# An encoder layer in float32 on one core: another weight split, other queues and another order in its seven-product stages

## Chip, cores and metric

The kernel runs on 1 core of one Trainium2 chip. The metric is the device time of one execution in microseconds; smaller is better. The engines are named as in the profile: PE (TensorE), DVE (VectorE), ACT (ScalarE), POOL (GpSimd) and SP (SyncE, which here only issues DMAs).

## What is computed

One layer of an encoder trunk over 1024 tokens of width 2048: RMSNorm, one input projection, grouped-query attention (8 query heads, 2 key heads) beside a bidirectional state-space part, then three products that this change is about, an output norm and a per-layer gate.

```python
y_ssm = jax.nn.gelu(y_ssm).astype(x.dtype)
glu = y_ssm @ w_glu[i] + b_glu[i]                       # (1024,1024) @ (1024,2048)
y_ssm = glu[..., :D_SSM] * jax.nn.sigmoid(glu[..., D_SSM:])
y_ssm = y_ssm * jax.nn.silu(gate_s)
h = h + jnp.concatenate([y_attn, y_ssm], axis=-1) @ w_out[i]   # (1024,2048) @ (2048,2048)
gate = jax.nn.sigmoid(rms_norm(h, norm_ple[i]) @ w_ple_gate[i])
h = h + gate * (p[i] @ w_ple_proj[i])
```

## The kernel before, in words

Data lie transposed: features on partitions, tokens along the free axis, in halves of 512. A float32 product is made of three matmuls on parts rounded to a shorter type: each operand is split into a high part H and a low part L = x - H, and HH + HL + LH is summed in PSUM. `split` (line 306) does it: ACT copies x to H with rounding (line 310; with a scale, line 313), DVE subtracts (line 311; line 314). `split_pool` (line 316) does both on POOL.

The program is written out in one order by hand, and each engine runs its instructions in that order. Helpers that run in pieces (generators) are put in a list with `bg`; `tick` (line 270) runs each of them one piece further, and takes one entry from the queue of fills `fq` if it is due. In the stages below the queue is `paced`: only three ticks of five take one (line 277). `put` (line 1090) issues the DMA of a moving tile `st` and appends its fill (its split) to be due `wait` ticks later.

After attention, `back` (line 1426) runs three stages of eight units: the gated product with w_glu (units 0 to 7), then w_out over the attention half (units 8 to 15), then over the other half (units 16 to 23). A unit multiplies a 2 x 2 block of weights, two tiles of 128 output features, with seven products instead of eight (Strassen's scheme in Winograd's form). The moving sides of the seven products are halves of the source or sums of them that `t_make` (line 1118) makes on POOL beforehand; `put_product` (line 1152) puts the four tiles of one. The weight sides are four blocks A11 to A22 and four sums of them: `sw_prep` (line 438) splits the next weights, three products ahead of use (`sw_next`, line 468), and `sw_sum` (line 432) makes the sums on POOL. `unit` (line 1165) runs 7 x 4 x 3 = 84 matmuls (lines 1176 to 1178) with a tick after each four-fold step's three matmuls, so four ticks per product and 28 per unit. After each product its PSUM tile (`pr`, four buffers) goes to `u_glu` (line 1191) or `u_out` (line 1238), which add it up: DVE adds at lines 1209 to 1226 and 1256 to 1281, POOL adds of SBUF tiles at lines 1210, 1221 and 1248. In the third stage `close` also squares each result (ACT, line 1264) and sums the squares (POOL, line 1265).

A `hook` after each product loads ahead: after product 6 of a stage's seventh unit and products 0 to 5 of its eighth, the next stage's products are put one by one. In the last unit it is the 14 first tiles of the gate stage (`put_h`), and the first three gate weights (`w_dma`, line 384; split by `w_split`, line 390).

The gate stage (`gate`, line 1392) multiplies two token halves with 16 blocks each: 48 matmuls `pg` (lines 1302 to 1304) and 6 matmuls `pp` per block. Before the second half its 16 tiles are put: nine in blocks 12 to 14, seven after the matmuls of block 15.

The stages begin while attention ends: `run` puts product 0 of the first stage six blocks before attention's last one, products 1, 2 and 3 later, products 4 to 6 after attention. Its loads share SP's queue with the store of the last attention output (line 1083).

Of the kernel before, what the change touches and what calls it, by code (L numbers as in the profile page):

```python
# [9 lines left out]
F32 = mybir.dt.float32  # L10
# [228 lines left out]
class Kernel:  # L239
# [30 lines left out]
    def tick(self):  # L270
        self.nt += 1
        for g in list(self.bgs):
            try:
                next(g)
            except StopIteration:
                self.bgs.remove(g)
        if self.fq and self.fq[0][0] <= self.nt and (not self.paced or self.nt % 5 in (0, 2, 4)):
            self.fill(*self.fq.pop(0)[1:])
# [153 lines left out]
    def sw_sum(self, u, o, a, b, op):  # L432

        if o not in self.sr and isinstance(o[1], str):
            self.sr[o] = self.wp.tile([128, 512], F32, name="wraw", tag="wraw", bufs=3)
        self.nc.gpsimd.tensor_tensor(self.sr[o], self.sr[a], self.sr[b], op)

    def sw_prep(self, g):
# [6 lines left out]
        L = self.wp.tile([128, 4, 128], F32R, name="wL", tag="wL", bufs=4)  # L445
        self.split(H, L, self.sr[src].rearrange("p (k m) -> p k m", m=128))
        self.shl[g] = (H, L)
# [703 lines left out]

    def put_product(self, X, i, s, src, **kw):
        for k in range(4):
            a = {
                0: src[k][:, 0:512],
                1: src[k + 4][:, 0:512],
                2: self.d_t[s][k][1][:, 512:1024],
                3: self.d_t[s][k][0][:, 512:1024],
                4: self.d_t[s][k][0][:, 0:512],
                5: src[k + 4][:, 512:1024],  # L1160
                6: self.d_t[s][k][1][:, 0:512],
            }[i]
            self.put(X, (i, k), a, **kw)

# [26 lines left out]
    def u_glu(self, n):  # L1191
# [27 lines left out]
        nc.vector.scalar_tensor_tensor(u1, ps, bv, u1, ALU.add, ALU.add)  # L1219
        nc.scalar.activation(g1, g1, AF.Sigmoid, bias=bg)  # L1220
        nc.gpsimd.tensor_tensor(v(g1), v(g1), rev(gs[:, h1]), ALU.mult)
        ps = yield
        nc.vector.tensor_tensor(u1, ps, u1, ALU.add)
        nc.vector.tensor_tensor(v(gs[:, h1]), rev(u1), rev(g1), ALU.mult)
        ps = yield
        nc.vector.tensor_tensor(u2, ps, u2, ALU.add)
        nc.scalar.activation(u2, u2, AF.Sigmoid, bias=bg)
        self.bg(self.u_glu_end(n, gs, v(gs[:, h0]), rev(v0), rev(u2)))
        yield

    def u_glu_end(self, n, gs, o, a, b):
        yield
        self.nc.vector.tensor_tensor(o, a, b, ALU.mult)
        for _ in range(5):
            yield
        self.nc.sync.dma_start(self.d_ms[n], gs)

    def u_out(self, m, src, dst, sq):
# [14 lines left out]
        def close(x, h, ps):  # L1253
# [3 lines left out]
            if not sq:  # L1257
                return
            acc = self.xsq[:, h]
            if m == 0 and x is r[0 if h is h0 else 1]:  # L1260
                nc.scalar.activation(acc, x[:, h], AF.Square)
            else:
                s2 = self.t2k("tq")
                nc.scalar.activation(s2, x[:, h], AF.Square)
                nc.gpsimd.tensor_tensor(acc, acc, s2, ALU.add)

# [24 lines left out]

    def mm_half(self, ps, nk, xs):

        nc = self.nc
        for k in range(nk):
# [9 lines left out]
            if k % 2:  # L1305
                self.tick()

    def h_rstd(self):
# [88 lines left out]
    def gate(self, hf, hg, nhg):  # L1397
# [5 lines left out]
        for n in range(16):  # L1403
# [7 lines left out]
            if hf == 0 and 12 <= n < 15:  # L1411
                self.put_h(nhg, 1, range(3 * n - 36, 3 * n - 33))
            self.mm_half(pg, 16, hg)
            if hf == 0 and n == 15:
                self.put_h(nhg, 1, range(9, 16))
            pp = self.psC("pp")
# [7 lines left out]
    def back(self, X):  # L1424
# [6 lines left out]
        hg = {}  # L1431
# [4 lines left out]
        for n, (s, u, thread) in enumerate(units):  # L1436

            def hook(i):
                if u < 7:
                    if u == 6 and i == 6:  # L1440
                        if s < 2:
                            self.put_product(nX, 0, s + 1, stages[s + 1][0])
                        else:
                            self.put_h(hg, 0, range(5))
                elif s < 2:
                    if i < 6:
                        self.put_product(nX, i + 1, s + 1, stages[s + 1][0], wait=8)
                else:
                    if i < 2:
                        self.put_h(hg, 0, range(5 + 4 * i, 9 + 4 * i), wait=8)  # L1450
                    elif i == 2:
                        self.put_h(hg, 0, [13], wait=8)
                    elif i == 3:
                        self.w_end = len(self.wq)
                        for _ in range(2):
                            self.w_dma()
                    elif i == 5:
                        self.w_dma()
                        for _ in range(2):
# [25 lines left out]
    def run(self):  # L1485
# [68 lines left out]
        for b in self.attention():  # L1554
# [9 lines left out]
            elif b == NB - 4 or b == NB - 2:  # L1564
                self.put_product(X, (b - NB + 6) // 2, 0, self.d_y2, pool=True, wait=2)
            elif b == NB + 1:
                self.put_product(X, 3, 0, self.d_y2, wait=2)
            elif b == NB + 2:
                self.sw_prep(0)
            elif b == NB + 3:  # L1570
                self.sw_prep(1)
        for i in range(4, 7):
            self.put_product(X, i, 0, self.d_y2, wait=3)
        self.back(X)
# [97 lines left out]
```

## Time and profile before

| | us |
|---|---|
| three timed runs | 2172.76, 2176.38, 2178.88 (median 2176.38) |
| the profiled execution's own time | 2172.48 |
| its span, first to last instruction | 2170.6 |
| mean granted TensorE clock in it | 0.986 |

Times in the profile count from the span's start. Attention ends and unit 0 begins at 1226.8, the second stage at 1389.5, the third at 1553.2; the last unit's matmuls end at about 1729.5, and the gate stage follows to the end. A granted clock of 1.00 is 2.4 GHz, 0.5 is 1.2 GHz. A matmul's modelled length overlaps the next one, so a busy PE is not a PE at its peak.

### The profile page before, as it was taken

To read this page: it belongs to the slowest core of one execution; us is meant where nothing else is said; L and a number is where in the kernel's file an instruction comes from. 1 tells how busy PE (TensorE), PEld (TensorE's weight loads), DVE (VectorE), ACT (ScalarE), POOL (GpSimd) and SP (SyncE) were. 2 spreads that over 40 slices of the span, in tenths; PEclk is the share of its full clock that TensorE was granted. 3 is DMA by queue.
4 is the path that set the end of the run, shared out by engine and by line. 5 is a ranking of instruction groups with operands and counts; after the bars stand their busy time and mean duration, and the time that the engine had idled before them with its cause. 6 is when DMAs were issued, how large, how long until landed. Compare 5 with 4: busy or idle time off the path is not lost. (4 is left out here: it accounts for less than half of the span.)

```text
span 2170.6 us, 29380 instructions
## 1 busy us (share of the span) xinstructions
PE 2076.4 (96%) x10140; PEld 1717.4 (79%) x10140; DVE 1496.1 (69%) x2394; ACT 798.7 (37%) x1454; POOL 965.1 (44%) x837
## 2 busy tenths in 40 slices
PE   8999999999999999999999899999989799999996
PEld 6888878888878888778888778778767678877885
DVE  7654787778878787749999867866766643455434
ACT  7111322222322222447777632522433343344332
POOL 0143456555556565504312467498478711221222
PEclk9999999999999999999999999999999999999998
DMA  5323223233232232554312545757835444455433
GB/s 214 92 99 101 80 83 105 82 99 87 88 101 80 82 109 72 173 190 153 126 40 79 187 173 174 271 201 257 293 121 170 155 136 127 128 185 165 142 114 126
DMA packets 183123, 296.47 MB, mean 137 GB/s; under 512 B 28352, under 2 KB 78656, under 8 KB 182720
## 3 DMA queue, kind: packets, MB, share of 16 engines
q1 hardware_dynamic: 181824, 292.51, 41.5%
q8 instruction: 80, 1.31, 0.3%
q10 hardware_dynamic: 1152, 2.10, 0.3%
q14 instruction: 67, 0.55, 0.1%
HBM read 211.37 MB, written 77.92 MB: 133 GB/s over the span
## 5 line engine op out<-in xcount | busy, mean ns | idle before, releaser
L311 DVE TENSOR_TENSOR wL<-wraw,wH 128x512 fp32r<-128x512 f32 (+1 forms) x352 | 305.3, 884 | 360.5 <-ACT wH L310 355.2
L310 ACT CAST wH<-wraw 128x512 fp32r<-128x512 f32 (+1 forms) x352 | 205.3, 598 | 344.1 <-DMA wraw<-in_w_gate_dram 98.1
L1177 PE MATMUL pr<-st,wH 128*128 128x512 f32 x672 | 267.3, 398 | 15.6 <-DVE st L311 15.6
L1176 PE MATMUL pr<-st,wH 128*128 128x512 f32 x672 | 266.0, 396 | 12.0 <-DVE cx L1256 7.9
L1178 PE MATMUL pr<-st,wL 128*128 128x512 f32 x672 | 265.3, 395 | 0.2
L1302 PE MATMUL pg<-st,wH 128*128 128x512 f32 x512 | 202.0, 394 | 9.2 <-ACT wH L310 7.9
L1303 PE MATMUL pg<-st,wH 128*128 128x512 f32 x512 | 201.4, 393 | 2.7 <-DVE st L314 2.6
L1304 PE MATMUL pg<-st,wL 128*128 128x512 f32 x512 | 200.8, 392 | 0.3 <-DVE wL L311 0.2
L1330 POOL TENSOR_TENSOR h<-cx,tz 128x512 f32<-128x512 f32 x31 | 40.4, 1303 | 297.5 <-DVE tz L1328 297.5
L1177 PEld LDWEIGHTS pr<-st,wH 128*128 128x128 f32 x672 | 127.8, 190 | 49.0 <-DVE st L311 23.2
L1176 PEld LDWEIGHTS pr<-st,wH 128*128 128x128 f32 x672 | 127.9, 190 | 44.6 <-issue 8.7
L1178 PEld LDWEIGHTS pr<-st,wL 128*128 128x128 f32 x672 | 128.2, 191 | 28.0 <-DVE wL L311 1.9
L311 DVE TENSOR_TENSOR wL<-sraw,wH 128x512 fp32r<-128x512 f32 x120 | 120.2, 1002 | 41.2 <-ACT wH L310 41.1
L892 ACT COPY ks<-kp 16x224 f32<-16x224 f32 x32 | 10.7, 335 | 335.3 <-DVE ks L891 208.7
L1248 POOL TENSOR_TENSOR cx<-cx,tz 128x512 f32<-128x512 f32 x64 | 102.1, 1606 | 64.5 <-DVE tz L1277 54.6
L1302 PEld LDWEIGHTS pg<-st,wH 128*128 128x128 f32 x512 | 96.8, 189 | 32.2 <-ACT wH L310 8.7
L1303 PEld LDWEIGHTS pg<-st,wH 128*128 128x128 f32 x512 | 96.9, 189 | 25.2 <-DVE st L314 5.0
L1304 PEld LDWEIGHTS pg<-st,wL 128*128 128x128 f32 x512 | 96.7, 189 | 21.8 <-DVE wL L311 1.8
L765 POOL TENSOR_TENSOR tab<-pa 128x512 f32<-128x512 f32 x32 | 41.4, 1292 | 159.5 <-DVE r L900 159.5
L310 ACT CAST wH<-sraw 128x512 fp32r<-128x512 f32 x120 | 73.0, 616 | 94.2 <-PE pr L1177 59.7
L574 PE MATMUL zga<-hH,wH 128*128 128x512 f32 x256 | 104.4, 408 | 0.0
L574 PE MATMUL zgs<-hH,wH 128*128 128x512 f32 x256 | 102.7, 401 | 0.6 <-ACT wH L310 0.6
(370 smaller groups left out, 5406.4 us busy)
## 6 DMA issues: line engine op xcount, KB each, us to landing
wraw<-in_w_in_dram SPq DMA_DIRECT2D x144, 256.0 KB
wraw<-in_w_gate_dram SPq DMA_DIRECT2D x128, 256.0 KB
sraw<-in_w_out_dram SPq DMA_DIRECT2D x64, 256.0 KB
st<-d_t SPq DMA_DIRECT2D x48, 256.0 KB
sraw<-in_w_glu_dram SPq DMA_DIRECT2D x32, 256.0 KB
cx<-in_xT_dram SPq DMA_DIRECT2D x16, 512.0 KB
d_p<-cx SPq DMA_DIRECT2D x16, 512.0 KB
cx<-d_p SPq DMA_DIRECT2D x16, 512.0 KB
```

The costliest lines, as they stand in the source:

```text
L310: nc.scalar.copy(H, src)
L311: nc.vector.tensor_tensor(L, src, H.bitcast(F32), ALU.subtract)
L574: nc.tensor.matmul(ps[h], H[:, kk, :], rH[:, s], start=(k == 0), stop=False)
L765: gp.tensor_tensor(out, x[:, :, None, :].to_broadcast(sh), pw[:, :, :, None].to_broadcast(sh), ALU.mult)
L1176: nc.tensor.matmul(ps, H[:, k], x[0], start=(k == 0), stop=False)
L1177: nc.tensor.matmul(ps, H[:, k], x[1], start=False, stop=False)
L1178: nc.tensor.matmul(ps, L[:, k], x[0], start=False, stop=(k == 3))
L1248: nc.gpsimd.tensor_tensor(x[:, h], x[:, h], u, ALU.add)
L1302: nc.tensor.matmul(ps, H[:, k % 4], x[0], start=(k == 0), stop=False)
L1303: nc.tensor.matmul(ps, H[:, k % 4], x[1], start=False, stop=False)
L1304: nc.tensor.matmul(ps, L[:, k % 4], x[0], start=False, stop=(k == nk - 1))
L1330: eng.tensor_tensor(hp, ho, t, ALU.add)
```

## The change

`sw_prep` copies H of each weight once more, on ACT into a PSUM tile `hp` (in the two buffers that attention's scores used), and DVE subtracts that copy instead of H. `sw_sum` runs on DVE for the weights of units 18 to 22. Fills are taken at four ticks of five, and in the second and third stage's puts four of the 28 tiles are split on POOL. In `u_glu` sigmoid and what follows it become pieces of their own, a tick or more apart; in `close` the square comes two ticks after the addition and its sum a tick later. At the start, products 3 and 4 are put during attention's last blocks, product 5 after it and product 6 after unit 0's first product. At the end the three gate weights are loaded from unit 22's last product on, and the seven last tiles of the second half are put within block 15.

```diff
-        if self.fq and self.fq[0][0] <= self.nt and (not self.paced or self.nt % 5 in (0, 2, 4)):
+        if self.fq and self.fq[0][0] <= self.nt and (not self.paced or self.nt % 5 != 4):
...
-        self.nc.gpsimd.tensor_tensor(self.sr[o], self.sr[a], self.sr[b], op)
+        eng = self.nc.vector if 18 <= u < 23 else self.nc.gpsimd
+        eng.tensor_tensor(self.sr[o], self.sr[a], self.sr[b], op)
...
-        self.split(H, L, self.sr[src].rearrange("p (k m) -> p k m", m=128))
+        raw = self.sr[src].rearrange("p (k m) -> p k m", m=128)
+        hp = self.ps.tile([128, 4, 128], F32, name="hp", tag="A", bufs=2)
+        self.nc.scalar.copy(H, raw)
+        self.nc.scalar.copy(hp, H.bitcast(F32))
+        self.nc.vector.tensor_tensor(L, raw, hp, ALU.subtract)
...
-    def put_product(self, X, i, s, src, **kw):
+    def put_product(self, X, i, s, src, share=False, **kw):
...
+            if share:
+                kw["pool"] = (4 * i + k) % 7 == 6
...
         nc.vector.scalar_tensor_tensor(u1, ps, bv, u1, ALU.add, ALU.add)
-        nc.scalar.activation(g1, g1, AF.Sigmoid, bias=bg)
-        nc.gpsimd.tensor_tensor(v(g1), v(g1), rev(gs[:, h1]), ALU.mult)
+        def half_1():
+            yield
+            nc.scalar.activation(g1, g1, AF.Sigmoid, bias=bg)
+            yield
+            nc.gpsimd.tensor_tensor(v(g1), v(g1), rev(gs[:, h1]), ALU.mult)
+            for _ in range(5):
+                yield
+            nc.vector.tensor_tensor(v(gs[:, h1]), rev(u1), rev(g1), ALU.mult)
+        def half_0():
+            yield
+            nc.scalar.activation(u2, u2, AF.Sigmoid, bias=bg)
+            yield
+            yield
+            nc.vector.tensor_tensor(v(gs[:, h0]), rev(v0), rev(u2), ALU.mult)
+            for _ in range(5):
+                yield
+            nc.sync.dma_start(self.d_ms[n], gs)
+        self.bg(half_1())
...
             nc.vector.tensor_tensor(x[:, h], ps, x[:, h], ALU.add)
             if not sq:
                 return
+            yield
+            yield
...
                 nc.scalar.activation(s2, x[:, h], AF.Square)
+                yield
                 nc.gpsimd.tensor_tensor(acc, acc, s2, ALU.add)
...
-            self.mm_half(pg, 16, hg)
             if hf == 0 and n == 15:
-                self.put_h(nhg, 1, range(9, 16))
+                self.mm_half(pg, 16, hg, lambda k: k < 15 and self.put_h(nhg, 1, [9 + k // 2], wait=3))
...
+                if n == 0 and i == 0:
+                    self.put_product(X, 6, 0, self.d_y2)
...
+                            self.w_end = len(self.wq)
+                            self.w_dma()
                             self.put_h(hg, 0, range(5))
...
-                        self.put_product(nX, i + 1, s + 1, stages[s + 1][0], wait=8)
+                        self.put_product(nX, i + 1, s + 1, stages[s + 1][0], wait=8, share=True)
...
+                        if i == 1:
+                            self.w_dma()
+                            self.w_dma()
...
-                    elif i == 3:
-                        self.w_end = len(self.wq)
-                        for _ in range(2):
-                            self.w_dma()
                     elif i == 5:
-                        self.w_dma()
...
+            elif b == NB:
+                self.put_product(X, 3, 0, self.d_y2, wait=2)
             elif b == NB + 1:
-                self.put_product(X, 3, 0, self.d_y2, wait=2)
+                self.put_product(X, 4, 0, self.d_y2, wait=2)
...
-        for i in range(4, 7):
-            self.put_product(X, i, 0, self.d_y2, wait=3)
+        self.put_product(X, 5, 0, self.d_y2, wait=6)
```

## Rows read from the trace of the kernel before

**Rows 1.** Page, part 1: busy time of each engine over the whole span.
```profile
PE 2076.4 (96%) x10140; PEld 1717.4 (79%) x10140; DVE 1496.1 (69%) x2394; ACT 798.7 (37%) x1454; POOL 965.1 (44%) x837
```

**Rows 2.** Windows: stretch, length; PE, PEld, DVE, ACT, POOL busy (instructions); clock; DMA.
```profile
1226.80:1275.30 48.50, 42.06 (x171) 32.81 (x170) 35.20 (x46) 19.09 (x33) 23.43 (x17) 0.93 0.58 207
...
1275.30:1389.50 114.20, 114.20 (x505) 94.64 (x504) 86.76 (x105) 41.32 (x73) 72.30 (x48) 1.00 0.62 210
...
1389.50:1438.90 49.40, 42.91 (x169) 31.82 (x168) 38.73 (x50) 17.97 (x33) 28.81 (x19) 0.97 0.60 207
...
1553.20:1607.10 53.90, 44.32 (x170) 33.42 (x169) 39.40 (x47) 22.16 (x40) 32.09 (x22) 0.91 0.52 181
...
1645.20:1729.50 84.30, 78.97 (x337) 61.97 (x335) 53.01 (x61) 32.61 (x57) 66.85 (x47) 1.00 0.52 172
...
1729.50:1759.40 29.90, 20.55 (x75) 13.94 (x74) 18.46 (x35) 11.06 (x19) 8.93 (x6) 0.83 0.36 119
...
1931.70:1944.00 12.30, 12.30 (x55) 10.14 (x54) 4.34 (x7) 3.95 (x7) 2.58 (x2) 1.00 0.45 128
...
1944.00:1962.30 18.30, 14.81 (x64) 10.68 (x62) 13.07 (x28) 11.53 (x19) 2.59 (x2) 1.00 0.57 204
```

**Rows 3.** Waits of PE, whole kernel: total us, times, longest.
```profile
PE pr L1177 <- DVE st L311: 15.6, 16, 2.4
...
PE pr L1176 <- DVE cx L1256: 7.9, 7, 3.1
...
PE pg L1302 <- ACT wH L310: 7.9, 2, 6.9
```

**Rows 4.** Lines 311 and 1256, units 0 to 23: ns shortest/median/longest.
```profile
L311 DVE TENSOR_TENSOR wL<-sraw,wH x119: 673/992/1814, 1228.0 to 1725.0; 128x512 fp32r<-128x512 f32 x119
...
L1256 DVE TENSOR_TENSOR cx<-pr,cx x64: 673/678/693, 1406.4 to 1740.3; 128x512 f32<-128x512 f32 x64
```

**Rows 5.** The window around unit 8, and DVE's timeline in it.
```profile
1375.10:1418.20 43.10, 36.61 (x149) 26.86 (x148) 41.06 (x55) 22.33 (x42) 19.80 (x11) 1.00 0.77 269
...
1388.42 5.19 DVE L311 TENSOR_TENSOR st<-st 128x512 fp32r<-128x512 f32 x3
...
1398.71 0.69 DVE L311 TENSOR_TENSOR wL<-sraw,wH 128x512 fp32r<-128x512 f32 x1 [1.30 <-ACT wH L310]
...
1402.83 1.88 DVE L311 TENSOR_TENSOR st<-st 128x512 fp32r<-128x512 f32 x3
```

**Rows 6.** ACT copies, SBUF to SBUF and PSUM to SBUF, as rows 4.
```profile
L310 ACT CAST wH<-sraw x118: 601/621/626, 1227.5 to 1724.4; 128x512 fp32r<-128x512 f32 x118
...
L1206 ACT COPY tz<-pr x8: 576/578/587, 1234.0 to 1373.8; 128x512 f32<-128x512 f32 x8
```

**Rows 7.** POOL: split, sum of weights (as rows 4); window of unit 22.
```profile
L318 POOL CAST st<-st x12: 609/618/811, 1181.6 to 1219.2; 128x512 fp32r<-128x512 f32 x12
...
L319 POOL TENSOR_TENSOR st<-st x12: 1262/1287/1300, 1182.3 to 1219.9; 128x512 fp32r<-128x512 f32 x12
...
L436 POOL TENSOR_TENSOR sraw<-sraw x24: 1275/1728/1758, 1225.9 to 1710.5; 128x512 f32<-128x512 f32 x24
...
1684.90:1705.70 20.80, 19.86 (x86) 15.58 (x86) 12.13 (x15) 6.72 (x12) 17.96 (x13) 1.00 0.51 166
```

**Rows 8.** SP's timeline at unit 0: start, length of issue, what.
```profile
1229.02 0.32 SPq L1083 DMA_DIRECT2D d_o<-ga  x1
...
1238.35 2.30 SPq L429 DMA_DIRECT2D sraw<-in_w_glu_dram  x4
```

**Rows 9.** Timelines of ACT and of SP where the gate stage begins.
```profile
1735.36 0.63 ACT L1264 ACTIVATE tq<-cx 128x512 f32<-128x512 f32 x1 [6.06 <-DVE cx L1256]
...
1750.36 0.62 ACT L310 CAST wH<-wraw 128x512 fp32r<-128x512 f32 x1 [8.11 <-DMA wraw<-in_w_gate_dram]
...
1740.45 0.92 SPq L1189 DMA_DIRECT2D d_h<-cx  x2
...
1745.36 0.39 SPq L387 DMA_DIRECT2D wraw<-in_w_gate_dram  x1
```

More of the change, by code (lines that the diff above doesn't have):

```diff
@@ L1219, in u_glu @@
         nc.vector.scalar_tensor_tensor(u1, ps, bv, u1, ALU.add, ALU.add)
-        nc.scalar.activation(g1, g1, AF.Sigmoid, bias=bg)
-        nc.gpsimd.tensor_tensor(v(g1), v(g1), rev(gs[:, h1]), ALU.mult)
+        def half_1():
[16 more added lines that the diff above has]
+        self.bg(half_1())
         ps = yield
         nc.vector.tensor_tensor(u1, ps, u1, ALU.add)
-        nc.vector.tensor_tensor(v(gs[:, h1]), rev(u1), rev(g1), ALU.mult)
         ps = yield
         nc.vector.tensor_tensor(u2, ps, u2, ALU.add)
-        nc.scalar.activation(u2, u2, AF.Sigmoid, bias=bg)
-        self.bg(self.u_glu_end(n, gs, v(gs[:, h0]), rev(v0), rev(u2)))
+        self.bg(half_0())
         yield
[L1231 to L1236, printed above, removed]
     def u_out(self, m, src, dst, sq):
@@ L1290, in u_out, with mm_half @@
         yield
-    def mm_half(self, ps, nk, xs):
+    def mm_half(self, ps, nk, xs, each=None):
         nc = self.nc
@@ L1306, in mm_half @@
                 self.tick()
+                if each:
+                    each(k)
     def h_rstd(self):
@@ L1412, in gate @@
                 self.put_h(nhg, 1, range(3 * n - 36, 3 * n - 33))
-            self.mm_half(pg, 16, hg)
             if hf == 0 and n == 15:
-                self.put_h(nhg, 1, range(9, 16))
+                self.mm_half(pg, 16, hg, lambda k: k < 15 and self.put_h(nhg, 1, [9 + k // 2], wait=3))
+            else:
+                self.mm_half(pg, 16, hg)
             pp = self.psC("pp")
```

## Prediction, made blind

> **What bounds the kernel now.** I read the page first. TensorE is busy for 96% of the span [rows 1], so time can only come from the places where it isn't fed or runs at a lower clock. I looked for those next, in the windows by unit [rows 2]. A unit is 84 matmuls; the reader is to see that six units in a row take 114.2 us, 19.03 each, at a granted clock of 1.00, and that the other windows exceed that: units 0 and 1 by 48.5 - 38.1 = 10.4 us, units 8 and 9 by 11.3, units 16 and 17 by 15.8, units 20 to 23 by 84.3 - 76.1 = 8.2. The first two blocks of the gate stage's halves are long as well: 29.9 against 12.3 us for a plain block (part of it the 20 matmuls that only this block has), and 18.3 against 12.3. So at most about 45.7 + 14 + 5 = 65 us is to be had, 3% of the kernel. Part of it is clock: 1 - granted clock is 0.07, 0.03, 0.09 and 0.17 of the first three pairs and the gate window, or 3.4 + 1.5 + 4.9 + 5.1 = 15 us that TensorE ran at 1.2 GHz, each time after waits.
>
> Third, TensorE's waits say for whom [rows 3]: VectorE's splits of the moving operand (st), VectorE's additions that empty PSUM (cx), and at the gate ScalarE's wH. So VectorE's queue is late just where a stage begins. Why shows the view of its durations [rows 4]: the same 128x512 subtraction takes 0.68 us at best and up to 1.8 when both inputs lie in SBUF, and never over 0.69 when one lies in PSUM. In the stretch around unit 8 [rows 5] VectorE is busy 41.06 of 43.10 us with 55 instructions; undisturbed ones follow each other every 0.60 us (three in 1.88), so 33 us of it is work and 8 us is waiting inside instructions (three st splits in 5.19).
>
> **The change, part by part.** *Subtraction from PSUM.* Each of the 168 weight splits gets a ScalarE copy of H to PSUM. No row shows a SBUF to PSUM copy; its neighbours are SBUF to SBUF at 0.62 us and PSUM to SBUF at 0.58 [rows 6]. I take 0.6 and bound it by 0.5 and 1.2 (twice a neighbour): 7 per unit are 4 us (3.5 to 8.4) of ScalarE, which is busy 41.3 of 114.2 us in six units, 6.9 per unit. It stays idle half of the time, so in plain units the copy costs nothing. VectorE's part falls from about 1.0 us (median 0.99) to 0.68: 7 x 0.3 = 2 us less per unit. The chain to the weights grows by one copy and one hand-over, under 1.5 us, while a split is made three products ahead, 3 x 19.03/7 = 8.2 us.
>
> The port itself: VectorE instructions with two SBUF inputs lengthen to what GpSimd's instruction beside them takes [rows 4, 7], those with one do not. The Trainium skill, in "SBUF — State Buffer", section "Who interferes with whom", says that such an instruction and a GpSimd one that reads SBUF exclude each other for the whole instruction. The trace agrees for VectorE (1.81 us at most, against 1.76 for a GpSimd sum [rows 7]). By that rule it also speaks against two other parts, the fills shared to GpSimd and the sums given to VectorE, since each keeps two SBUF inputs; if each of the eight GpSimd instructions of the shared fills blocked in full (1.29 us instead of the 8/11 = 0.73 us found below), the transitions would lose about 4 us more apiece.
>
> *Fills at four ticks of five instead of three, 4 of 28 on GpSimd, sigmoid issued apart.* At a stage's end 28 fills are put for the next stage. A tick is a quarter product, 0.68 us. Counted from unit 7's first tick, the first fill is due at tick 6; at 0.6 per tick the last is issued at tick 52, at 0.8 at tick 41, and TensorE wants it at tick 55, 33 us after tick 6. Before, 55 instructions stood ahead of it: 33 us of work plus 8 inside waits plus 2 of gaps make 43, 10 late, and 11.3 was lost. After, 24 fills, 9 weight splits and 11 others are 44 x 0.60 = 26.4 us; waits inside I take as 9 (15 GpSimd instructions instead of 11, but 26 of 44 exposed instead of 42 of 55), gaps 1.5: 37, some 4 late. The other limit is the emptying of PSUM: an addition issued at tick 40 frees the bank that TensorE wants at tick 48, 5.4 us later, and VectorE is then 9 to 11 us behind: 4 to 6 late. I take 5.5 left at unit 8 and 7 at unit 16: gains 6 and 9. Bounds: nothing left (11 and 16), or no gain, if the waits inside grow as far as the work shrinks. The four GpSimd fills are 4 x (0.62 + 1.29) = 7.6 us [rows 7] beside its own work; they have 14 ticks or more of room. The sigmoid a tick later only reorders ScalarE's queue: nothing by itself.
>
> *Start of unit 0.* SyncE's queue stands at the last attention store until 1229.02, and the first weights of unit 1 go out only at 1238.35, behind products 4 to 6, twelve loads, and a gate tile: 0.7 us each [rows 8]. After, product 3's loads are issued one block and product 4's two steps earlier, ahead of that store; product 5's four remain behind it, and product 6's four pass behind the first weights. So four loads and one gate tile stand ahead of those weights, eight loads fewer, 5 us sooner. Products 3 and 4 are now split among the last attention blocks, where ScalarE waits for TensorE anyway; what they delay if not is the last transposes, by 0.6 us each at most for 5 fills. I take 8 of the 10.4 (5 to 10).
>
> *Sums on VectorE and squares later, third stage.* GpSimd is busy 17.96 of 20.8 us in unit 22 [rows 7], above 19.03 with any wait, and VectorE's additions wait for it, TensorE for them (7.9 us, [rows 3]). Taking four sums of 1.3 to 1.8 us [rows 7] away leaves 12. VectorE, at 12.1 us there, gets 4 x 0.7 to 1.8 and loses 2: 13 to 17, still under 19. Behind a sum that waits for its load stand the additions that empty PSUM; the loads go out more than two products ahead. Squares two ticks later no longer hold ScalarE's wH. Gain 6.5 of 8.2 (0 to 8).
>
> *Gate.* ScalarE's first gate wH stands behind a square that waited 6.06 us for VectorE's addition, and SyncE sends the fourth weight tile at 1745.36, behind stores that wait for the last additions until 1740.45 [rows 9]. After, the square comes behind the wH, the 14 fills are issued some 10 ticks sooner, and three weight loads go out a unit earlier (one ahead of five st loads, two ahead of four: 0.4 us of issue each, in a queue that afterwards stands until 1740.45 anyway). What is late next is that fourth tile: store, two reloads and its landing remain one chain, 1740.45 to 1750.36 at its split, some 10 us behind the last addition, against 12 x 3 x 0.227 = 8.2 us of matmuls that can run before it. Gain 6.5 (3 to 12).
>
> *Second half.* Seven loads and fills spread over block 15 instead of after it. The block that wants them takes 18.3 instead of 12.3 us, with nine matmuls more [rows 2], so some 4 to 5 us of it are waits; I take 3.5 (0 to 5).
>
> **The sum.** 8 + 6 + 9 + 6.5 + 6.5 + 3.5 = 39.5 us. The profiled execution took 2172.5 us (span 2170.6), 3.9 below the median 2176.4; taken from the median: 2137.
>
> **Rivals.** (1) *VectorE stays the bound at the transitions*, since fills on GpSimd and fills on VectorE block each other: 15 us of gain fall away, at worst some of unit 0's: 2152 to 2165. For it: 8 us inside waits today; against it: fewer exposed instructions and earlier issue. (2) *Slower: ScalarE loses its lead.* The PSUM copies have two buffers, freed by VectorE's subtraction two splits earlier, so ScalarE can't run further ahead of VectorE. If each of the 28 fills then pays a ScalarE to VectorE hand-over like the 1.30 us gap of [rows 5], about 1 us, that is 28 us per transition and 12 at unit 0: 68 against 39.5 gained, 2205. It decides once VectorE is over two products, 5.4 us, late throughout; against it, two splits ahead still means some six fills in hand. (3) *No change*: the subtraction stays long although H is in PSUM, and the lateness moves elsewhere; 64 of 64 additions with a PSUM input under 0.70 us speak against it: 2170 to 2180.
>
> **How the numbers follow.** The forecast, each term within its bounds, 2119 to 2150: 0.70. Rival 1: 0.19. Rival 3: 0.06. Rival 2: 0.05. The range is 2118 to 2161: below lies only the case that nearly all 65 us go, above rivals 2 and 3 and the rest of 1. About 0.3%, 6.5 us, can be told from no change in this kernel: faster 0.89, same 0.06, slower 0.05.
>
> **What would show it.** Right: weight subtractions at 0.68 us with no tail; units 0, 8 and 16 at 20 to 25 us instead of 28 to 34; units 20 to 23 at 19; the gate's first block near 23; no half clock at unit 0 and shorter ones elsewhere; VectorE still without pause around units 7 to 9. Wrong: subtractions still up to 1.8 us; ScalarE idle before its PSUM copies for VectorE; a plain unit, such as 3 or 12, above 19.1; or long waits for VectorE's sums in units 18 to 22.

## The result, and the profile after

The changed kernel takes 2138.73 us (median of four runs, 2136.98 to 2141.96) against 2177.63 us for the kernel before on the same chip: a ratio of 0.9826, with a 95% interval of 0.9805 to 0.9848. It is faster, and 1.7 us from the forecast. The profiled executions differ by less, 2135.8 against 2170.6 us of span, 34.8 us. The table sets that difference against the terms of the prediction; a stretch runs from the start of its first matmul to the start of the next stretch's, except that the wait ahead of the gate's first matmul counts with the gate.

| stretch | before, us | after, us | gain forecast | gain measured |
|---|---|---|---|---|
| units 0 and 1 | 48.5 | 41.1 | 8 | 7.4 |
| units 8 and 9 | 49.4 | 48.1 | 6 | 1.3 |
| units 16 and 17 | 53.9 | 44.8 | 9 | 9.1 |
| units 20 to 23 | 84.4 | 76.2 | 6.5 | 8.2 |
| gate: wait and first block | 29.9 | 25.7 | 6.5 | 4.2 |
| first block of the second half | 18.3 | 13.4 | 3.5 | 4.9 |
| later start of unit 0 (0.55), other blocks | | | 0 | -0.3 |
| sum | | | 39.5 | 34.8 |

Part 1 of the page, as [rows 1]: VectorE has lost 27 us of work and ScalarE has taken on 99 (168 PSUM copies of 0.59 us).

```profile
PE 2062.8 (97%) x10140; PEld 1716.9 (80%) x10140; DVE 1469.1 (69%) x2406; ACT 897.7 (42%) x1614; POOL 919.1 (43%) x833
```

The windows that answer to [rows 2], with the same columns: units 0 and 1, 8 and 9, 16 and 17, 20 to 23, the gate's first block, and the second half's. (Those of units 20 to 23 and of the gate lie up to 0.5 us beside the table's stretches.)

```profile
1227.35:1268.50 41.15, 39.08 (x171) 31.16 (x170) 31.48 (x45) 28.71 (x49) 20.62 (x16) 1.00 0.60 205
1382.70:1430.80 48.10, 42.19 (x169) 33.43 (x168) 36.39 (x49) 26.67 (x47) 32.26 (x25) 0.93 0.61 207
1545.10:1589.90 44.80, 40.44 (x170) 32.45 (x169) 37.39 (x49) 27.68 (x49) 33.87 (x25) 0.96 0.65 216
1628.00:1704.60 76.60, 76.29 (x337) 62.84 (x335) 54.88 (x73) 49.86 (x86) 48.53 (x35) 1.00 0.57 189
1704.64:1730.30 25.66, 19.71 (x76) 13.63 (x77) 14.39 (x32) 9.58 (x17) 6.29 (x4) 0.93 0.44 139
1914.50:1927.90 13.40, 13.40 (x64) 10.97 (x63) 9.83 (x23) 7.64 (x14) 3.04 (x2) 1.00 0.48 150
```

Five of the six are clearly shorter than in [rows 2] (a plain pair of units is 38.1 us). The second, units 8 and 9, is not, and it is the only one whose granted clock fell, from 0.97 to 0.93. Much of what follows is about that line.

TensorE's waits, as [rows 3], over the whole kernel (`L1183` to `L1185` are now the matmuls of a unit, `L1322` to `L1324` those of the gate):

```profile
PE pr L1183 <- DVE cx L1273: 7.1, 3, 2.8
...
PE pg L1324 <- DVE wL L311: 3.6, 1, 3.6
PE pr L1183 <- DVE tz L1251: 3.1, 1, 3.1
...
PE pr L1183 <- DVE tz L1219: 1.9, 1, 1.9
...
PE pg L1322 <- ACT wH L310: 1.0, 2, 0.6
...
PE pr L1184 <- DVE st L311: 0.2, 1, 0.2
```

The 15.6 us of waits for fills (`st`) are down to 0.2, the gate's 7.9 us for `wH` to 1.0. What is left in the units are waits for VectorE's additions that empty PSUM, 12.1 us in five waits, and at the gate one of 3.6 us for `wL`.

Durations by line (ns shortest/median/longest): the weight subtraction with the PSUM operand (`L451`), the PSUM copy, POOL's additions in `u_out`, and POOL's two instructions of a shared fill.

```profile
L451 DVE TENSOR_TENSOR wL<-sraw,hp x120: 670/686/690, 1226.3 to 1697.1; 128x512 fp32r<-128x512 f32 x120
...
L450 ACT COPY hp<-wH x168: 589/591/592, 1225.5 to 1695.1; 128x512 f32<-128x512 f32 x168
...
L1265 POOL TENSOR_TENSOR cx<-cx,tz x64: 1282/1297/1831, 1396.6 to 1705.5; 128x512 f32<-128x512 f32 x64
...
L318 POOL CAST st<-st x20: 607/808/1083, 1182.0 to 1558.5; 128x512 fp32r<-128x512 f32 x20
...
L319 POOL TENSOR_TENSOR st<-st x20: 1263/1295/1802, 1182.7 to 1559.7; 128x512 fp32r<-128x512 f32 x20
```

The subtraction's tail is gone: 690 ns at most against 1814 in [rows 4].

Now unit 8, to be read beside [rows 5]. First a window of 42 us around its start:

```profile
1368.00:1410.00 42.00, 36.09 (x143) 28.38 (x142) 40.81 (x50) 27.38 (x50) 24.46 (x18) 0.92 0.76 262
```

VectorE's timeline in it:

```profile
1388.62 3.40 DVE L311 TENSOR_TENSOR st<-st 128x512 fp32r<-128x512 f32 x3
1391.94 1.74 DVE L1235 TENSOR_TENSOR cx<-tz,tq 128x512 f32<-128x512 f32 x1
1393.60 0.68 DVE L1251 TENSOR_TENSOR tz<-pr,tz 128x512 f32<-128x512 f32 x1
...
1396.79 1.78 DVE L1242 TENSOR_TENSOR cx<-tq,tz 128x512 f32<-128x512 f32 x1
```

POOL in the same stretch (sums of weights `L437`, then a shared fill, `L318` and `L319`):

```profile
1388.62 1.84 POOL L437 TENSOR_TENSOR sraw<-sraw,wraw 128x512 f32<-128x512 f32 x1
1390.40 1.07 POOL L318 CAST st<-st 128x512 fp32r<-128x512 f32 x1
1391.55 1.58 POOL L319 TENSOR_TENSOR st<-st 128x512 fp32r<-128x512 f32 x1
```

And TensorE, waiting for the addition at 1393.60 of the lines above:

```profile
1394.43 0.47 PE L1183 MATMUL pr<-st,wH 128*128 128x512 f32 x1 [3.12 <-DVE tz L1251]
...
1404.62 0.47 PE L1183 MATMUL pr<-st,wH 128*128 128x512 f32 x1 [2.79 <-DVE cx L1273]
```

Right behind each of these two waits TensorE runs for 3.4 us at a granted clock of 0.5, 1.2 GHz, which loses it 1.7 us each time:

```profile
1394.90:1398.30 3.40, 3.40 (x9) 2.69 (x9) 3.30 (x4) 3.37 (x8) 1.68 (x2) 0.51 0.27 80
...
1405.20:1408.60 3.40, 3.40 (x10) 2.62 (x9) 3.40 (x7) 0.59 (x1) 1.65 (x2) 0.50 0.38 67
```

VectorE is busy 40.81 of 42.00 us with 50 instructions, 0.82 us each; before it was 41.06 us with 55, 0.75 each [rows 5]. It took the long weight subtractions out of this stretch and got longer ones elsewhere: fills, and two multiplications of SBUF tiles (`L1235`, `L1242`) that last 1.74 and 1.78 us beside POOL's instructions (0.69 and 0.68 in the kernel before). The addition that frees a PSUM bank stands behind them.

### The profile page after: what moved, and what is told of

The parts are those of the page before. It is cut to its first block, busy times and chain, and to the rows that moved or that the text cites. A ratio compares the mean times of both kernels' runs of the same rounds, so it can differ in the third digit from the quotient of the medians.

```text
span 2135.8 us, 29630 instructions
## 1 busy us (share of the span) xinstructions
PE 2062.8 (97%) x10140; PEld 1716.9 (80%) x10140; DVE 1469.1 (69%) x2406; ACT 897.7 (42%) x1614; POOL 919.1 (43%) x833
## 4 chain that ended last, share of the span: by engine, by line
PE 54%; DVE 9%; DMA 3%; ACT 2%; issue 1%; POOL 1%; SPq 1%; DVEq 0%; ACTq 0%; POOLq 0%
PE pr L1183 6%; PE pr L1184 6%; PE pr L1185 6%; PE pg L1322 5%; PE pg L1323 5%; PE pg L1324 5%; PE ptr L1015 2%; PE zgs L579 2%; PE zgs L582 2%; PE zgs L580 2%; DMA st<-d_t 1%; PE pv L1029 1%; PE pv L1028 1%; PE pv L1030 1%; PE S L985 1%
## 5 line engine op out<-in xcount | busy, mean ns | idle before, releaser
L311 DVE TENSOR_TENSOR wL<-wraw,wH 128x512 fp32r<-128x512 f32 x304 | 253.5, 852 | 297.5 <-ACT wH L310 294.0
L310 ACT CAST wH<-wraw 128x512 fp32r<-128x512 f32 x304 | 175.5, 595 | 264.5 <-DMA wraw<-in_w_gate_dram 98.5
L1183 PE MATMUL pr<-st,wH 128*128 128x512 f32 x672 | 264.2, 393 | 12.1 <-DVE cx L1273 7.1
L1185 PE MATMUL pr<-st,wL 128*128 128x512 f32 x672 | 263.8, 393 | 0.0
L1184 PE MATMUL pr<-st,wH 128*128 128x512 f32 x672 | 263.4, 392 | 0.2 <-DVE st L311 0.2
L1324 PE MATMUL pg<-st,wL 128*128 128x512 f32 x512 | 200.2, 391 | 3.6 <-DVE wL L311 3.6
L1322 PE MATMUL pg<-st,wH 128*128 128x512 f32 x512 | 200.9, 392 | 1.0 <-ACT wH L310 1.0
L1183 PEld LDWEIGHTS pr<-st,wH 128*128 128x128 f32 x672 | 127.3, 189 | 41.3 <-ACT hp L450 5.8
L1185 PEld LDWEIGHTS pr<-st,wL 128*128 128x128 f32 x672 | 127.3, 189 | 27.7 <-DVE wL L451 0.9
L1324 PEld LDWEIGHTS pg<-st,wL 128*128 128x128 f32 x512 | 96.5, 188 | 24.8 <-DVE wL L311 4.5
L1322 PEld LDWEIGHTS pg<-st,wH 128*128 128x128 f32 x512 | 96.5, 188 | 23.4 <-ACT wH L310 1.8
L1265 POOL TENSOR_TENSOR cx<-cx,tz 128x512 f32<-128x512 f32 x64 | 87.8, 1384 | 61.1 <-DVE tz L1297 40.7
L451 DVE TENSOR_TENSOR wL<-sraw,hp 128x512 fp32r<-128x512 f32 x120 | 81.9, 683 | 42.3 <-ACT hp L450 36.4
L770 POOL TENSOR_TENSOR tab<-pa 128x512 f32<-128x512 f32 x32 | 41.4, 1293 | 157.8 <-DVE r L905 157.8
L579 PE MATMUL zq<-hH,wH 128*128 128x512 f32 x256 | 103.3, 404 | 0.0
```

What stands on the lines that cost most here:

```text
L310: nc.scalar.copy(H, src)
L311: nc.vector.tensor_tensor(L, src, H.bitcast(F32), ALU.subtract)
L451: self.nc.vector.tensor_tensor(L, raw, hp, ALU.subtract)
L579: nc.tensor.matmul(ps[h], H[:, kk, :], rH[:, s], start=(k == 0), stop=False)
L1183: nc.tensor.matmul(ps, H[:, k], x[0], start=(k == 0), stop=False)
L1184: nc.tensor.matmul(ps, H[:, k], x[1], start=False, stop=False)
```

## The experiments

Times of single stretches are compared, since the time ahead of unit 0 differs by 7 us between two executions of the same kernel (below). Units 2 to 7, 10 to 15, 18 and 19 take 19.04 us in every run, but for one unit 4 with 0.1 to 0.7 us more where the PSUM operand is left out, and for what is told of the run without all three parts.

**1. The PSUM operand, taken out and alone.** The changed kernel with `sw_prep` as before:

```diff
-        hp = self.ps.tile([128, 4, 128], F32, name="hp", tag="A", bufs=2)
-        self.nc.scalar.copy(H, raw)
-        self.nc.scalar.copy(hp, H.bitcast(F32))
-        self.nc.vector.tensor_tensor(L, raw, hp, ALU.subtract)
+        self.split(H, L, raw)
```

> The changed kernel, but DVE subtracts H from SBUF again, and the PSUM copy is gone. Theory (the PSUM operand only spares DVE its waits beside POOL, 0.3 us per subtraction): units 8 and 16, where DVE is never idle, get 2 to 4 us longer each, unit 0 up to 1, the third stage 0 to 2, plain units stay at 19.04; in all 5 to 12 us more than the changed kernel, about 2147. Rival A (the PSUM operand carries most of the gain): 20 us or more lost, 2160. Rival B (the extra ACT copy costs as much as the subtraction saves): within 3 us of the changed kernel.

And the kernel before with that edit the other way round, and nothing else of the change:

> The kernel before, with the PSUM copy and the subtraction from it as its only change. Theory: DVE saves 0.3 us per weight subtraction where it is the bound: units 8 and 16 each 2 to 4 us shorter, unit 0 up to 2, the third stage's last units 0 to 3; 5 to 12 us less than before, about 2168. Rival A: 20 us less or more. Rival B (ACT, held by two PSUM buffers, loses its lead over DVE): no gain or slower, ACT idle before its PSUM copies in units 8 and 16.

Without the PSUM operand 2148.42 us, ratio 0.9874 [0.985, 0.9899], against 0.9826 with it: 9.7 us between the medians, of which the two profiles show 6.5 from unit 0 to the end. Unit 8 is 1.7 us longer, unit 16 2.4, the gate's first block 1.3; VectorE is then busy 41.80 of the 42.00 us around unit 8. Alone it gives 2165.51 us, ratio 0.9949 [0.9932, 0.9965], some 11 us by the medians and 8.9 by the profiles from unit 0 on; 8.2 come from units 20 to 23, which then take 76.2 us, and 2.2 from units 16 and 17, while unit 8 is 2.3 us longer than before and units 0 and 1 together 1.2. So the part works, but it does not shorten units 0 and 8 by itself.

**2. The fills shared with GpSimd, given back to VectorE.**

```diff
-                        self.put_product(nX, i + 1, s + 1, stages[s + 1][0], wait=8, share=True)
+                        self.put_product(nX, i + 1, s + 1, stages[s + 1][0], wait=8)
```

> The changed kernel, with all 28 fills of a transition on ACT and DVE, none on POOL. Theory (the four POOL fills hold up DVE's fills through the SBUF port, which is why unit 8 still takes 29.1 us): unit 8 falls to 25 to 27 us, unit 16 by 0 to 3, 2 to 6 us less in all. Rival (unit 8 is bound by the mere number of DVE instructions, and POOL takes four away): units 8 and 16 get 2 to 3 us longer each, 4 to 6 us more in all.

2132.12 us, ratio 0.9798 [0.9775, 0.9822]. The interval overlaps the changed kernel's, but from unit 0 to the end this profile is 5.9 us shorter. Unit 8 takes 23.5 us instead of 29.1, unit 16 25.1 instead of 25.8. The window:

```profile
1366.00:1408.00 42.00, 38.66 (x167) 30.69 (x167) 39.21 (x57) 32.62 (x59) 14.02 (x9) 1.00 0.79 273
```

VectorE's timeline, the last two lines at a place shown above:

```profile
1384.24 4.73 DVE L311 TENSOR_TENSOR st<-st 128x512 fp32r<-128x512 f32 x3
...
1390.09 1.88 DVE L311 TENSOR_TENSOR st<-st 128x512 fp32r<-128x512 f32 x3
1391.90 0.68 DVE L1235 TENSOR_TENSOR cx<-tz,tq 128x512 f32<-128x512 f32 x1
```

TensorE's waits from 1375 to 1415:

```profile
PE pr L1183 <- DVE cx L1273: 1.7, 1, 1.7
PE pr L1185 <- DVE wL L451: 1.4, 1, 1.4
PE pr L1183 <- ACT wH L449: 0.2, 1, 0.2
```

VectorE executes seven instructions more in the same 42 us and is busy 1.6 us less: 0.69 us each instead of 0.82. Three fills take 1.88 us where they took 3.40, the multiplication 0.68 instead of 1.74; three others, a little earlier, still take 4.73, so it is the mean that tells. The granted clock stays at 1.00. POOL has 9 instructions there instead of 18. The work taken off VectorE, four subtractions of 0.60 us or 2.4 in all, was paid for with 5.8 us in longer instructions (10.8 us beyond 0.60 for each instruction with the shared fills, 5.0 without them). The Trainium skill says so in "Perfetto Trace Analysis", section "Optimizing Scalar/DVE Operations": moving work between VectorE and GpSimd might not help, since they share a port. This pair of runs agrees, with 5.6 us.

Of these 5.6 us 3.4 are the clock's: 0.92 instead of 1.00 over 42 us. At unit 16 the clock goes the other way. The windows of 42 us around it, with shared fills and without:

```profile
1530.00:1572.00 42.00, 37.64 (x158) 30.11 (x157) 39.23 (x48) 27.17 (x50) 28.25 (x21) 0.96 0.82 281
...
1525.00:1567.00 42.00, 39.11 (x161) 31.78 (x160) 37.97 (x54) 30.40 (x55) 18.47 (x13) 0.92 0.85 293
```

There 1.7 us are lost to the clock with the shared fills and 3.4 without them. With the clock's share taken out, the shared fills cost 2.2 us at unit 8 and 2.4 at unit 16.

**3. The third stage: which part freed units 20 to 23.** The sums back on GpSimd; then also the PSUM operand out, so that the later squares stand alone; then the squares back as well:

```diff
-        eng = self.nc.vector if 18 <= u < 23 else self.nc.gpsimd
+        eng = self.nc.gpsimd
...
-            yield
-            yield
             acc = self.xsq[:, h]
...
                 nc.scalar.activation(s2, x[:, h], AF.Square)
-                yield
                 nc.gpsimd.tensor_tensor(acc, acc, s2, ALU.add)
```

> The changed kernel, with all sums of weights on POOL again. Theory (POOL's load sets the pace of the third stage): units 20 to 23 together lose 5 to 9 us again, as before (84.3 us instead of 76.2), unit 16 changes by under 1; about 2145. Rival (the squares issued later took POOL and ACT out of the chain, the sums matter little): units 20 to 23 stay within 1 us of 76.2.

> The changed kernel, with H subtracted from SBUF again and all sums of weights on POOL again: of the three edits that touch the third stage's pace (PSUM operand, sums on DVE, squares issued later) only the squares are left. With the PSUM operand alone units 20 to 23 took 76.2 us, and without it too. Theory (any one of the three takes 1.7 us out of a loop of 20.7 us per unit): units 20 to 23 stay within 1 us of 76.2, units 8 and 16 as without the PSUM operand, 30.8 and 28.2; about 2148. Rival (the squares alone don't suffice; PSUM operand or sums are needed): units 20 to 23 take 80 us or more, 2153 or more.

> The changed kernel without three of its parts at once: weights subtracted from SBUF, sums of weights all on GpSimd, squares right behind the addition. Each part alone left units 20 to 23 at 76.2 us. Theory (any one of the three is enough, and nothing else is): units 20 to 23 return to 82 to 85 us, units 0 to 7 and 8 to 15 as without the PSUM copy, and the median is 2152 to 2162. Rival (something else of the change does it, the other pace of fills or the weight loads at the end): units 20 to 23 stay at 76 to 77 us and the median is 2147 to 2150.

Sums on GpSimd: 2141.57 us, ratio 0.9839 [0.9818, 0.986], with units 20 to 23 at 76.2 us as in the changed kernel. Squares later as the only one of the three: 2148.65 us, ratio 0.9862 [0.9839, 0.9885], again 76.2 us. None of the three: 2165.12 us (two runs), ratio 0.9947 [0.9929, 0.9965], and units 20 to 23 at 87.3 us, 2 us beyond the range expected; here units 16 to 19 lose 1.1 to 2.5 us each as well, which made the median longer than expected. So the PSUM operand alone (experiment 1) and the later squares alone are each enough, and something of the three is needed; sums on VectorE alone were not tried. Why, shows POOL. A window of one unit's length without any of the three:

```profile
1659.90:1680.60 20.70, 19.82 (x86) 15.53 (x85) 12.03 (x15) 6.72 (x12) 17.86 (x13) 1.00 0.47 152
```

The waits of POOL, ScalarE and VectorE in units 20 to 22 of that run (`L1261` is POOL's addition, `L1269` VectorE's closing one, `L1277` the square, `L1278` its sum):

```profile
POOL xsq L1278 <- ACT tq L1277: 4.6, 3, 1.5
POOL cx L1261 <- DVE tz L1290: 3.7, 3, 1.2
...
ACT tq L1277 <- DVE cx L1269: 34.3, 12, 4.0
...
DVE cx L1269 <- POOL cx L1261: 3.6, 3, 1.2
```

And a window of that kind with the later squares alone, then one with the PSUM operand alone:

```profile
1659.90:1678.94 19.04, 19.04 (x85) 15.77 (x84) 10.76 (x14) 7.11 (x13) 17.99 (x13) 1.00 0.51 167
...
1663.70:1682.74 19.04, 19.04 (x85) 15.77 (x84) 9.05 (x15) 11.10 (x19) 15.16 (x13) 1.00 0.51 166
```

POOL's work is the same in the first two, 17.9 and 18.0 us, and in the second it fits into 19.04 us with no loss. What cost 1.66 us a unit was a round: POOL's queue stands 1.5 us at the sum for ScalarE's square, which waits for VectorE's closing addition, which waits for an addition of POOL's; and behind the sum the next addition is late. A square issued later breaks the round, and so does slack on POOL: with the PSUM operand alone its work is 15.2 us a unit.

The gate shows a second effect of the square: without any of the three, TensorE waits 7.88 us before the gate's first matmul; with the later squares alone 0.41. The first block is longer for it, 27.18 us instead of 21.98, so 2.3 us of it are a gain.

**4. The start: order of loads, or pace.** Products 3 to 6 put where they were before; then pace three of five (without shared fills) with the new order; then the old order and the old pace together:

```diff
-                if n == 0 and i == 0:
-                    self.put_product(X, 6, 0, self.d_y2)
...
-            elif b == NB:
-                self.put_product(X, 3, 0, self.d_y2, wait=2)
             elif b == NB + 1:
-                self.put_product(X, 4, 0, self.d_y2, wait=2)
+                self.put_product(X, 3, 0, self.d_y2, wait=2)
...
-        self.put_product(X, 5, 0, self.d_y2, wait=6)
+        for i in range(4, 7):
+            self.put_product(X, i, 0, self.d_y2, wait=3)
...
-        if self.fq and self.fq[0][0] <= self.nt and (not self.paced or self.nt % 5 != 4):
+        if self.fq and self.fq[0][0] <= self.nt and (not self.paced or self.nt % 5 in (0, 2, 4)):
```

> The changed kernel, with products 3 to 6 of the first stage put where they were before. Theory (the loads' place in SyncE's queue is what made unit 0 shorter): units 0 and 1 get 5 to 8 us longer again, 41.1 to 46 to 49; the rest unchanged; about 2145. Rival (pace and PSUM operand shortened unit 0): within 2 us of the changed kernel.

> The changed kernel without fills on POOL, and with fills at three ticks of five as before. Theory (four of five is needed, since at three of five the last fill is issued three ticks before TensorE wants it): units 8 and 16 get 2 to 5 us longer each than the 23.5 and 25.1 without fills on POOL, about 2138. Rival (slower pace leaves DVE free to empty PSUM in time, which is what TensorE waits for): units 8 and 16 stay or get shorter, 2132 or less.

> The changed kernel with products 3 to 6 of the first stage put where they were before, and with three ticks of five taking a fill. Either of the two parts alone left units 0 and 1 at 40.1 to 41.4 us. Theory (pace and order of loads replace each other): units 0 and 1 take 46 to 50 us; units 8 and 16 also lose some 3 us each to the slower pace, and the median is 2150 to 2158. Rival (the sigmoid issued apart, or the PSUM copy, is what shortens units 0 and 1): they stay at 40 to 42 us and the median is 2142 to 2149.

| | units 0 and 1 | 8 and 9 | 16 and 17 | median, us | ratio |
|---|---|---|---|---|---|
| the changed kernel | 41.1 | 48.1 | 44.8 | 2138.73 | 0.9826 |
| old order | 41.4 | 48.2 | 44.8 | 2142.37 | 0.9832 [0.981, 0.9854] |
| pace three of five, no shared fills | 40.1 | 48.2 | 47.1 | 2143.52 | 0.9837 [0.9811, 0.9862] |
| old order and pace three of five | 48.3 | 52.0 | 53.5 | 2156.89 | 0.9909 [0.9886, 0.9933] |

Either part is enough for unit 0, and without both its loss is back. It was not the late weights: with the old order the weights of unit 1 go out 11.8 us after unit 0's start (1232.5), late as before [rows 8], and TensorE waits for none of them. SP's line with the old order:

```profile
1244.28 2.31 SPq L429 DMA_DIRECT2D sraw<-in_w_glu_dram  x4
```

TensorE's waits in units 0 and 1 with the old order, all of them:

```profile
PE pr L1184 <- DVE st L311: 2.3, 3, 0.9
```

The same waits with the old order and the old pace:

```profile
PE pr L1183 <- ACT st L310: 2.7, 2, 1.6
PE pr L1184 <- DVE st L311: 2.1, 4, 0.9
```

They are waits for fills, of both engines: with twelve of them outstanding at unit 0's start and three ticks of five they are issued too late; at four of five, or with fewer outstanding, in time or nearly so. From these waits come two stretches of 3.4 us at a granted clock of 0.5, 1.2 GHz, in that run, and none in the run above. The queue of loads may have a share in the lateness: behind unit 0's start ScalarE waits for the load of a fill, 3.44 us with the old order and 4.22 with the old pace as well. That wait does not decide alone: in the changed kernel ScalarE waits 3.69 us for such a load too, and TensorE only 0.2 us for a fill. The queue's share was not taken apart. At units 8 and 16 the slower pace costs 5.6 and 3.0 us against experiment 2, and the waits at unit 8 turn from `DVE cx`, one of 1.7 us, into `DVE st`, 4.0 us in five. With the shared fills, the second row against the fourth, it costs 3.8 and 8.6 us.

**5. A faster version.** Without shared fills, the next stage's first product, and the gate's first five tiles, put five products earlier; then the gate's fourth and fifth weight tile also sent ahead of the last two stores; and beside it the changed kernel again on the same chip:

```diff
-                    if u == 6 and i == 6:
+                    if u == 6 and i == 1:
                         if s < 2:
                             self.put_product(nX, 0, s + 1, stages[s + 1][0])
                         else:
-                            self.w_end = len(self.wq)
-                            self.w_dma()
                             self.put_h(hg, 0, range(5))
+                    elif u == 6 and i == 6 and s == 2:
+                        self.w_end = len(self.wq)
+                        self.w_dma()
...
         self.paced = False
+        self.w_dma()
+        self.w_dma()
         while self.bgs:
```

> The changed kernel without fills on POOL, and with the next stage's first product (and the gate's first five tiles) put five products sooner, in unit 6's second step, where DVE has time. Theory (the transitions are bound by the number of DVE instructions between the first fill and TensorE's want): four of 28 fills, 2.4 us and what they wait, leave that stretch: units 8 and 16 get 2 to 4 us shorter each than 23.5 and 25.1, the gate's first block 2 to 4 us shorter than 25.6; about 2123. Rival (what is left are single late items: the split of a weight, a PSUM copy, which come after the fills anyway): within 2 us of 2132.

> The kernel of the run with the earlier first products and no shared fills, with one more edit: the fourth and the fifth weight tile of the gate are sent before the last unit's additions are drained, so ahead of the last two stores. Theory (the fourth tile's chain of store, two reloads and landing holds the gate's first block): that tile's split no longer waits for a DMA, block 0 of the gate takes 20 to 21.5 us instead of 22.6, and the median is 1 to 2 us under the run it comes from, 2130 to 2132. Rival (the additions and the splits on VectorE hold it, the tile only lands among them): block 0 stays within 0.5 us of 22.6, and the first reload of the residual, now behind two loads, makes nothing else late; the median is 2132 to 2134.

> The changed kernel itself, unedited, on the same chip as the runs beside it, so that the faster version can be compared with it directly: 2136 to 2142 us, 0.982 to 0.984 of the kernel before, and 5 to 9 us above the run beside it with the gate's weights sent earlier.

The first: 2132.51 us, ratio 0.9787 [0.9765, 0.9809], 9.5 us over what was expected. Against experiment 2 unit 16 gained 2.3 us, 1.7 of them by the clock, and the gate's wait and first block 1.25; unit 8 lost 0.9, no more than it differs between this run and the next (24.4 and 23.2 us), whose further edit does not touch it. So the first fills were not, in the main, what the rest waits for. The second: 2130.31 us, ratio 0.9793 [0.9775, 0.9811], beside the changed kernel's 2141.98, ratio 0.9842 [0.9824, 0.9861], on the same chip. The intervals don't touch: this version beats both kernels, by 46 and by 11.7 us. From unit 0 to the end its profile is 8.6 us shorter than the change's, 5.9 of them those of the fills that are not shared. The gate's edit itself gave nothing: the first block takes 22.97 us after 22.62, as its rival had it. ScalarE's line for the fourth tile in the changed kernel:

```profile
1720.40 0.62 ACT L310 CAST wH<-wraw 128x512 fp32r<-128x512 f32 x1 [8.40 <-DMA wraw<-in_w_gate_dram]
```

and with the tile sent earlier:

```profile
1704.86 0.62 ACT L310 CAST wH<-wraw 128x512 fp32r<-128x512 f32 x1 [0.30 <-DMA wraw<-in_w_gate_dram]
```

TensorE's waits around that run's start of the gate:

```profile
PE pg L1324 <- DVE wL L311: 2.0, 1, 2.0
PE pg L1322 <- ACT wH L310: 1.4, 1, 1.4
```

The wait of ScalarE is gone, and TensorE's for `wL` is not.

The changed kernel again ran 2142.0 here and 2138.7 before. Its two profiles differ by 6.9 us of span, and unit 0 starts 7.0 us later in the second (1234.4 for 1227.35); from there on they agree. Medians of runs on different chips are therefore read to some 4 us only.

## Why the prediction was right, and where it was not

The sign and the size were right (39.5 us forecast, 38.9 between the medians). That the median came within 1.7 us of the forecast is in part luck: between the two profiled executions it was 34.8, and the medians of the changed kernel itself differ by 3.2 us (experiment 5). The 4.7 us missing in the profiles are the shortfall of unit 8, and that the errors of the other terms, up to 2.3 us, cancel is luck too. Rivals 2 and 3 did not come: ScalarE's copy kept its lead (plain units stayed at 19.04 us), and the subtraction did get short. Of the signs that the prediction named, unit 8 (29.1 us for 20 to 25) and the gate's first block (25.2 for 23) did not come, and unit 16 (25.8) just missed. Four of the reasons need mending.

- **Subtraction from PSUM: right.** 0.69 us at most for all 168; the copy cost 0.59 us against 0.6 taken; taken out, 6.5 us of the gain go by the profiles and 9.7 by the medians. The saving reaches POOL too, which the prediction did not count: the longest of its additions in `u_out` fell from 3489 to 1831 ns, the median from 1678 to 1297. It is this part that does it: with the PSUM operand alone they take 1304 (1843) ns, and with it alone taken out 1672 (3486). The rule cited from the Trainium skill, "SBUF — State Buffer", section "Who interferes with whom", agrees in both directions with these rows: VectorE's two-input instructions of SBUF tiles reach 1.78 us beside GpSimd, those with an operand in PSUM never.
- **Unit 8, the term that failed (6 us forecast, 1.3 measured).** The forecast left 5.5 us of loss at this unit, and the waits were of that size, 3.1 and 2.8 us. What it put at nothing was the clock: behind each of the two waits TensorE ran 3.4 us at 1.2 GHz, 1.7 us of work lost each time. Together these are 9.3 of the 10.0 us that unit 8 is over plain. Without shared fills the clock did not fall, the unit is 5.6 us shorter, and units 8 and 9 take 42.6 us, a gain of 6.8 where 6 was forecast. So it was these fills that made the term fail, 2.2 us by waits and 3.4 by the clock that fell behind them. The step "waits inside I take as 9" came to 40.81 - 50 x 0.60 = 10.8 us in the window, and to 39.21 - 57 x 0.60 = 5.0 without shared fills. Its price held: 5.8 us for eight GpSimd instructions are the 0.73 us each that it took, and not the 1.29 of the dearer alternative. Its count did not: four shared fills are eight instructions, so 11 of before become 19 and not 15, and the window has 18. Rival 1, VectorE as the bound because the fills block each other, came true at this transition, and only in part.
- **Pace: right as the cause, and larger than its place in the text.** It is what carries units 8 and 16 (5.6 and 3.0 us in experiment 4 without shared fills, 3.8 and 8.6 with them).
- **Unit 16: right (9 forecast, 9.1).** Shared fills cost only 0.7 us here, although VectorE's mean is as long (39.23 us for 48 instructions in the 42 us around it). The difference from unit 8 is the clock's: without it they cost 2.4 us here and 2.2 there (experiment 2).
- **Start: right in size (8 forecast, 7.4), wrong in its main cause.** "SyncE's queue stands" was the reason given, and the late first weights of unit 1. Old order, same gain: TensorE did not wait for those weights. What ended the loss was that fewer fills were outstanding, or that they were issued sooner, and either does it; the queue's share in the lateness of the fills stays open.
- **Third stage: right in size (6.5, 8.2), wrong in cause.** "GpSimd is busy 17.96 of 20.8 us in unit 22 [rows 7], above 19.03 with any wait" took a busy engine for the bound. The same 18 us run in 19.04 when the wait of its queue for the square is gone. Sums on VectorE were not needed.
- **Gate: 4.2 for 6.5.** The part on the square held, though only 2.3 us of it are net. The fourth weight tile came as late as forecast, 10.2 us from the store at 1710.20 to its split at 1720.40, but TensorE lost only 0.65 us by it. The larger remaining wait, 3.65 us for `wL`, was not foreseen, nor the clock of 0.93 in this window, another 1.8 us of work lost. VectorE's lines ahead of it:

```profile
1700.69 4.15 DVE L314 SCALAR_TENSOR_TENSOR st<-st,vec 128x512 fp32r<-128x512 f32 x3
1704.76 0.68 DVE L1301 TENSOR_TENSOR tz<-pr,tz 128x512 f32<-128x512 f32 x1
1705.36 2.40 DVE L314 SCALAR_TENSOR_TENSOR st<-st,vec 128x512 fp32r<-128x512 f32 x2
1707.69 0.68 DVE L1273 TENSOR_TENSOR cx<-pr,cx 128x512 f32<-128x512 f32 x1
1708.29 1.28 DVE L311 TENSOR_TENSOR wL<-wraw,wH 128x512 fp32r<-128x512 f32 x2
```

  Five fills beside POOL's last additions take 6.55 us instead of five times 0.6 to 0.7, and the weight subtraction of the gate, whose operand `w_split` leaves in SBUF, comes behind them. That an earlier issue of these fills helps is bounded by experiment 5, 1.25 us; the blocking itself was not taken away here.
- **Second half: 4.9 for 3.5**, within its bounds; it was not tried apart.

Two numbers of the working are read wrongly. The 15 us that it calls time at 1.2 GHz are the time lost by it: at half the clock, 0.93 over 48.5 us is 6.8 us at 1.2 GHz and 3.4 lost, so the four stretches together are some 30 us. And 2119 to 2150 is not what the bounds of the terms add up to: taken together they allow gains of 8 to 62 us, 2114 to 2168.

## What to carry to other kernels

Where VectorE is the late engine, count how long its instructions take beside GpSimd's before handing GpSimd a part of its work: four subtractions of 0.6 us moved over cost TensorE 2.2 and 2.4 us at two stage starts here, and 3.4 more at the one where its clock fell behind the waits, while one more ScalarE copy that puts an operand into PSUM freed both engines. An engine that is busy 94% of a period is not yet its bound; look at whom its in-order queue stands for, and issue the waited-for instruction later. And when a change has several parts, take each out alone and then all of them together: parts that replace each other show nothing when only one is removed.

## What was not expected of the hardware

- The blocking is mutual, and reaches GpSimd's instructions with one input: its cast takes 0.61 us undisturbed and 1.07 to 1.08 beside VectorE's instructions with two SBUF tiles around unit 8 (`L318` above).
- TensorE's granted clock fell to 1.2 GHz for 3.4 us after single waits of about 3 us (1394.9 and 1405.2, right behind the two waits shown), so a wait of 3 us cost 4.8. In the run without shared fills, with waits of 1.7 us and less at that place, it stayed at 2.4 GHz. The length of one wait does not decide it: at unit 0 with the old order and pace it fell behind several waits, the longest of 1.6 us.
- ScalarE's copy from SBUF to PSUM took 0.59 us for 128x512, a little less than the 0.62 of its copy from SBUF to SBUF, which also rounds [rows 6].
